# First block of a two-block model on one core: the gate and convolution projections computed by seven block products per pair of weight tiles, with gated sums kept in DRAM between phases

## The chip, the core and the metric

The kernel runs on one core of a Trainium2 chip. The metric is the device time of one execution in microseconds (us). The engines in the text: PE multiplies matrices (its weight loads are listed apart as PEld), DVE is the vector engine, ACT the scalar (activation) engine, POOL the GpSimd engine, SP the engine whose queue issues most loads. "hi" and "lo" are the two parts into which an fp32 operand is split, so that a product in reduced precision is made in three passes.

## The reference

Input x has 1024 tokens with 1024 features. The first block, cut to what the change touches:

```python
h = rmsnorm(x, norm_g)
q, k, v, z_att, gb, gc, u, z_conv, g_att, g_conv = split(h @ w_in)
att    = chunked_rel_attention(q, k, v, rel_bias)
y_att  = (att * silu(z_att)) @ w_att_out          # 512 -> 1024
vconv  = causal_depthwise_conv(gc * u)            # width 3
y_conv = (gb * vconv * silu(z_conv)) @ w_conv_out # 512 -> 1024
m = sigmoid(g_att) * y_att + sigmoid(g_conv) * y_conv
x = x + m @ w_out
```

rmsnorm(x, g) is x times a factor r per token (one over the root of the mean square) times the gain g. A final norm, a second block (a sparse-attention mixer, a cross attention and a gated feed-forward part, FFN, with 2816 hidden features) follow.

## The kernel before, in words

**Layout.** Activations lie transposed: 128 features on the partitions, 1024 tokens along the row, so 8 tiles make 1024 features. A weight tile is 128x1024 and holds eight 128x128 blocks, one for each tile of input features. `w` (line 173) loads one into the single buffer "wr"; ACT copies it to a hi tile ("wh"), DVE subtracts for the lo tile ("wl"). `dense_full` (line 202) makes 128 output features: 8 feature tiles (4 when the input has 512 features), two token halves and three passes (hi by hi, lo by hi, hi by lo: `mm3`, line 190), so 48 (or 24) matmuls of 128x512, into a PSUM tile "S".

**Buffers.** Named by tag, [128, 1024] fp32 each: U (32), P (6), PT (4), wr (1), wh and wl (2 each). PSUM: S (2 tiles, 1024 wide), T (2), A and D (1 each). A buffer is given out again in turn when its last reader is done. "spill" is a write to DRAM from POOL's queue (`dspill`, line 168), "reload" a read from there on SP's queue. A load may be tied to an earlier matmul (`ago`), so that it does not start too soon. Each engine takes its instructions in order; a scheduler sets that order from the program and its own estimates, except on PE inside `manual_schedule`, where the order of the program text holds.

**First block** (`block1`, line 675). The normed x (without the factor r: it is a row R over the tokens and is multiplied in afterwards, `times_R`) is held as 8 hi/lo pairs `hn` in 16 U buffers. Query, key, value and four pairs of heads are worked off; `z_gate` (line 578) makes for each pair the product att·silu(z) (`attg`) in hi/lo, which is spilled to DRAM and reloaded behind the last of them. Then:

- `rope_base` makes a sine and cosine table for the second block (into the tile "cs"), with 3 of ACT's changes of function table (sine, tanh) around it.
- `gates(28, "wao", attg, True)`: for each of 8 output tiles a gate product (w1[28+d], 48 matmuls), times R, tanh, and the y_att product (wao, 24 matmuls), combined to mt[d].
- a loop over 4 tiles with four products each (w1[16+d], [20+d], [12+d], [24+d]: gc, u, gb, z_conv), with the convolution and the gating between them, to `convg`.
- `gates(36, "wco", convg, False)`: the same for the convolution branch, added to mt[d].
- mt split to hi/lo (`ms`), and 8 products with wo1, to which x is added.

**The FFN of the second block** has another scheme, which the change takes over. Two weight tiles of 128 output features are done together. The 1024 input features are taken as two halves and the two output tiles as two, a 2x2 block product, and likewise the tokens in two halves of 512; sums of blocks are made first, so that seven products of 12 matmuls each (`product`, P1 to P7) take the place of eight: 84 matmuls instead of 96. `operands` (line 1473) makes the right-hand sums from the activations once (7 U tiles for each of 4 pairs of feature tiles), `left_x` and `left_y` (lines 1497, 1504) make the left-hand ones for every weight pair (on DVE and ACT, in wh, wl, PT and U buffers). `begin` runs P1 of a pair, `end` the others, with P1 of the next pair between P7 and P4; ACT or DVE takes partial results out of PSUM between them. In the FFN, R is multiplied in behind the products.

Of the kernel before, what the change touches and what calls it, by code (L numbers as in the profile page):

```python
# [98 lines left out]
class Kernel:  # L99
# [568 lines left out]
    def block1(self):  # L668
# [40 lines left out]
        self.rope_base()  # L709
        mt = [self.big("U" if d < 6 else "P") for d in range(8)]  # L710
        whole = slice(0, 1024)

        def gates(c0, wname, src, first):
            wy = None
            for d in range(8):
                g = self.dense_full(I["w1"][c0 + d], hn)
                th = self.times_R(g, whole, "P")
                self.act(th, th, AF.Tanh, scale=0.5)
                if d % 2 == 0:
                    wy = self.w(I[wname][d // 2])  # L720
                y = self.dense_full(None, src, w=wy, wo=(d % 2) * 512)
                if first:
                    self.stt(mt[d], th, 1.0, y, OP.add, OP.mult)
                else:
                    self.stt(th, th, 1.0, y, OP.add, OP.mult)
                    self.tt(mt[d], mt[d], th, OP.add)

        gates(28, "wao", attg, True)
        convg = []
        R2 = self.big("PT")  # L730
        self.act(R2, self.R, AF.Square)
        for d in range(4):
            gc = self.dense_full(I["w1"][16 + d], hn)
            u1 = self.big("PT")
            self.act(u1, gc)
            u = self.dense_full(I["w1"][20 + d], hn)
            self.tt(u1, u, u1, OP.mult)
            self.tt(u1, u1, R2, OP.mult)
            t0 = self.big("P")
            cw = lambda j: self.gvec[:, GV["cw1"] + 4 * j + d:GV["cw1"] + 4 * j + d + 1]  # L740
            self.act(t0, u1, AF.Identity, scale=cw(2), bias=self.gv("cb1", d))
            self.stt(t0[:, 1:], u1[:, :1023], cw(1), t0[:, 1:], OP.mult, OP.add)
            self.stt(t0[:, 2:], u1[:, :1022], cw(0), t0[:, 2:], OP.mult, OP.add)
            gb = self.dense_full(I["w1"][12 + d], hn)
            self.tt(t0, t0, gb, OP.mult)
            self.nc.gpsimd.tensor_tensor(t0, t0, self.R, op=OP.mult)
            z = self.times_R(self.dense_full(I["w1"][24 + d], hn), whole)
            th = self.big("P")
            self.act(th, z, AF.Tanh, scale=0.5)
            self.stt(th, th, 1.0, z, OP.add, OP.mult)  # L750
            self.tt(t0, t0, th, OP.mult)
            hi, lo = self.big("U", F32R), self.big("U", F32R)
            self.split(hi, lo, t0, scale=0.5)
            convg.append((hi, lo))
# [968 lines left out]
```

## Time and profile before

| | |
|---|---|
| median of 3 runs | 2506.16 us (2504.4 to 2506.25) |
| the profiled execution | 2509.58 us, of which 2507.8 us are the span of the trace; mean granted PE clock 0.976 of full speed |
| PE busy in the span | 2384.4 us, 95% |
| gates and convolution branch, before the wo1 products | 316.39 to 757.54 us of the span |
| wo1 products | 757.54 to 845.83 us |
| FFN, one weight pair (of 22) | 19.29 us |

A line of an engine's timeline reads: start in us, length in us, engine, line of the kernel, operation, output<-inputs by buffer name, shape, count, and in brackets the idle time before it and what ended it. A row of a window reads: the stretch, its length, then PE, PEld, DVE, ACT and POOL busy time with (xcount), the granted PE clock as a share of full speed, the busy share of the DMA engines and GB/s. A row of the chain of waits: start, length, what the program's end waited for. A group's row ends in "busy us, mean ns of one | idle before".

### The profile page before, as it was taken

To read this page: it belongs to the slowest core of one execution; us is meant where nothing else is said; L and a number is where in the kernel's file an instruction comes from. 1 tells how busy PE (TensorE), PEld (TensorE's weight loads), DVE (VectorE), ACT (ScalarE), POOL (GpSimd) and SP (SyncE) were. 2 spreads that over 40 slices of the span, in tenths; PEclk is the share of its full clock that TensorE was granted. 3 is DMA by queue.
4 is the path that set the end of the run, shared out by engine and by line. 5 is a ranking of instruction groups with operands and counts; after the bars stand their busy time and mean duration, and the time that the engine had idled before them with its cause. 6 is when DMAs were issued, how large, how long until landed. Compare 5 with 4: busy or idle time off the path is not lost.

```text
span 2507.8 us, 32225 instructions
## 1 busy us (share of the span) xinstructions
PE 2384.4 (95%) x12516; PEld 2024.4 (81%) x12516; DVE 1527.3 (61%) x2502; ACT 1157.8 (46%) x1949; POOL 200.8 (8%) x302
## 2 busy tenths in 40 slices
PE   8999999999999999967878999999999999999999
PEld 7887878888888889966777787887878888888887
DVE  5476732333434469778966886444578888875443
ACT  4455521121223247687766774344445544553231
POOL 0000000001000014321211111000000000000000
PEclk9999999999999999988989999999999999999999
DMA  4323321111113332225343324311422222225454
GB/s 138 99 66 112 104 92 51 50 43 51 42 59 118 108 101 66 70 81 164 114 142 107 94 67 164 114 59 51 151 84 76 85 89 80 76 85 184 168 185 143
DMA packets 82328, 246.52 MB, mean 98 GB/s; under 512 B 10368, under 2 KB 15872, under 8 KB 82176
## 3 DMA queue, kind: packets, MB, share of 16 engines
q1 hardware_dynamic: 68256, 195.48, 24.6%
q0 software_dynamic: 13488, 48.77, 5.3%
q8 instruction: 98, 1.61, 0.3%
q10 hardware_dynamic: 432, 0.23, 0.1%
q14 instruction: 54, 0.44, 0.1%
HBM read 171.03 MB, written 51.90 MB: 89 GB/s over the span
## 4 chain that ended last, share of the span: by engine, by line
PE 75%; DVE 9%; issue 6%; ACT 5%; DMA 3%; POOL 2%; SPq 0%; DVEq 0%; POOLq 0%; ACTq 0%
PE S L186 46%; PE D L186 9%; PE T L186 9%; PE A L186 7%; PE T L490 2%; ACT jka L130 2%; DVE U L133 2%; DMA U<-sp 1%; DVE P L133 1%; ACT P L130 1%; DVE P L483 1%; POOL st L218 1%; DVE jkd L1117 1%; ACT U L130 1%; DVE PT L133 1%
## 5 line engine op out<-in xcount | busy, mean ns | idle before, releaser
L186 PE MATMUL S<-U,wh 128*128 128x512 f32 x2624 | 831.7, 392 | 16.4 <-ACT U L130 8.4
L186 PEld LDWEIGHTS S<-U,wh 128*128 128x128 f32 x2624 | 495.2, 189 | 122.5 <-ACT U L130 8.4
L186 PE MATMUL S<-U,wl 128*128 128x512 f32 x1312 | 513.4, 391 | 2.8 <-DVE wl L133 2.8
L130 ACT ACTIVATE wh<-wr 128x1024 fp32r<-128x1024 f32 (+1 forms) x144 | 145.7, 1011 | 579.1 <-PE S L186 354.8
L186 PEld LDWEIGHTS S<-U,wl 128*128 128x128 f32 x1312 | 247.9, 189 | 56.9 <-DVE wl L133 4.7
L133 DVE TENSOR_TENSOR wl<-wr,wh 128x1024 fp32r<-128x1024 f32 (+1 forms) x144 | 167.5, 1163 | 193.1 <-ACT wh L130 192.9
L186 PE MATMUL D<-U,wh 128*128 128x512 f32 x752 | 261.8, 400 | 0.3 <-DVE U L133 0.2
L186 PE MATMUL S<-U,U 128*128 128x256 f32 (+6 forms) x1040 | 217.3, 336 | 14.5 <-DVE st L483 13.6
L186 PEld LDWEIGHTS S<-U,U 128*128 128x128 f32 x1040 | 161.0, 201 | 31.2 <-DVE st L483 14.3
L186 PEld LDWEIGHTS D<-U,wh 128*128 128x128 f32 x752 | 140.8, 189 | 27.4 <-DVE U L133 1.5
L186 PE MATMUL D<-U,wl 128*128 128x512 f32 x376 | 149.1, 396 | 0.4 <-DVE wl L133 0.4
L130 ACT ACTIVATE P<-P,st 128x640 f32<-128x640 f32 (+7 forms) x168 | 124.0, 739 | 40.4 <-DVE st L483 38.9
L186 PE MATMUL S<-wh,U 128*128 128x256 f32 x768 | 142.7, 288 | 0.0
L130 ACT ACTIVATE PT<-T 128x512 fp32r<-128x512 f32 (+4 forms) x208 | 110.3, 544 | 53.4 <-PE T L490 46.0
L186 PE MATMUL S<-U,PT 128*128 128x512 f32 x528 | 130.1, 395 | 0.0
L186 PEld LDWEIGHTS S<-wh,U 128*128 128x128 f32 x768 | 122.7, 196 | 0.0
L186 PE MATMUL T<-U,wh 128*128 128x512 f32 x352 | 119.0, 390 | 0.0
L186 PEld LDWEIGHTS S<-U,PT 128*128 128x128 f32 x528 | 99.1, 188 | 23.7 <-ACT jkd L130 0.2
L186 PE MATMUL A<-PT,U 128*128 128x256 f32 (+2 forms) x448 | 110.8, 340 | 5.2 <-ACT PT L130 1.9
L130 ACT ACTIVATE jka<-U,C 128x768 int8<-128x768 f32 (+2 forms) x96 | 99.7, 1039 | 34.1 <-DVE C L136 29.5
L133 DVE TENSOR_TENSOR PT<-T,PT 128x512 fp32r<-128x512 f32 (+1 forms) x160 | 101.6, 646 | 22.5 <-ACT PT L130 20.6
L133 DVE TENSOR_TENSOR P<-S,R 128x512 f32<-128x512 f32 (+1 forms) x46 | 39.8, 872 | 120.0 <-PE S L186 120.0
(296 smaller groups left out, 4144.2 us busy)
## 6 DMA issues: line engine op xcount, KB each, us to landing
U<-sp SPq DMA_DIRECT2D x65, 512.0 KB, 4.1
sp<-U POOLq DMA_DIRECT2D x53, 512.0 KB, 3.7
wr<-in_w SPq DMA_DIRECT2D x43, 512.0 KB, 3.3
U<-in_wf SPq DMA_DIRECT2D x43, 512.0 KB, 3.6
P<-sp SPq DMA_DIRECT2D x42, 512.0 KB, 4.4
sp<-P POOLq DMA_DIRECT2D x38, 512.0 KB, 2.9
U<-U SPq DMA_DIRECT2D x116, 128.0 KB, 2.3
wr<-in_wf SPq DMA_DIRECT2D x23, 512.0 KB, 3.6
```

The source lines that it names most:

```text
L130: return self.nc.scalar.activation(out, in_, f, **kw)
L133: return self.nc.vector.tensor_tensor(out, a, b, op=op)
L186: self.last = self.nc.tensor.matmul(out, l, r, start=start, stop=stop, skip_group_check=True)
L218: self.nc.gpsimd.tensor_tensor(y, v, self.mhalf[:, :n], op=OP.pow)
L483: self.nc.vector.tensor_tensor_reduce(pv, v, add.rearrange("p (n x) -> p n x", n=n), scale, BIG, OP.add, OP.min, nm)
L490: self.nc.tensor.transpose(T[:, j * 128:j * 128 + 128], b, self.ident)
L1117: self.nc.vector.tensor_scalar(self.junk["d"][:, :w], SD[i], C[:, j:j + 1].bitcast(F32), None, op0=OP.is_lt, op1=OP.add, accum_out=cnt[:, ...
```

## The change

The part of `block1` between z_gate and the wo1 products becomes a new method `gates(attg)`. It does these things:

- All 32 weight tiles of the gates and the convolution loop go through the seven-product scheme, as 16 pairs (28/29 to 34/35 for the attention gate; 16+d/20+d and 12+d/24+d for the convolution; 36/37 to 42/43 for its gate). Right-hand sums are made from x itself, loaded anew (8 tiles), times the gain and times R; for the first four feature tiles in one DVE instruction, for the others by an ACT scaling and a POOL multiply by R. `hn` is no longer needed there, and `times_R` goes.
- The y_att products (wao) stand first. While they run, the right-hand sums are made. Their results go out of PSUM by ACT, in halves through the tiles cs and jkd, and to DRAM (16 DMAs of 256 KB on SP's queue). For j=0 two S tiles are filled together, feature tile by feature tile.
- Gated sums (M, 8), convolution results (4) and six of the eight tanh tiles of the second gate are spilled and reloaded between the phases; the y_att results are reloaded (8).
- The y_conv products (wco) stand last, in the order j = 3, 2, 1, 0, and ms[d] is split as each is made. The wo1 products begin at feature tile 4 (`rot=4`).
- z_gate(3) keeps its hi/lo in SBUF; attg[1] is reloaded into P buffers, attg[2] into PT buffers.
- `rope_base` stands behind the pair loop. PE's order is that of the text for the whole part.

Rows in the program's order (neighbouring instructions that read alike share one): PE 11504 before and 11248 after, of which 64 new ones stand for two matmuls each, so that there are 192 matmuls fewer; DVE 2342 and 2504; ACT 1514 and 1635; POOL 267 and 283; SP 530 and 578. Everything up to the last z_gate, and everything behind the first wo1 product, stands in the same order as before on every engine. Lines of the kernel from 168 on move by three.

SP's queue at the start of the part, with the reloads of attg (names with numbers: sp291/292 are attg[0], sp447/448 attg[1], sp599/600 attg[2], sp681/682 attg[3]). Before:

```order
L158 DMA U683_3293<-sp291_1632 128x1024
L158 DMA U684_3294<-sp292_1634 128x1024
L158 DMA U685_3297<-sp447_2294 128x1024
L158 DMA U686_3298<-sp448_2296 128x1024
L158 DMA U687_3301<-sp599_2948 128x1024
L158 DMA U688_3302<-sp600_2950 128x1024
L158 DMA wr714_3437<-in_w1 128x1024
L158 DMA U689_3305<-sp681_3289 128x1024
L158 DMA U690_3306<-sp682_3291 128x1024
```

After:

```order
L158 DMA U681_3289<-sp291_1632 128x1024
L158 DMA U682_3290<-sp292_1634 128x1024
L158 DMA PT685_3297<-sp599_2948 128x1024
L158 DMA PT686_3298<-sp600_2950 128x1024
L158 DMA P683_3293<-sp447_2294 128x1024
L158 DMA P684_3294<-sp448_2296 128x1024
L158 DMA P687_3303<-in_xT 128x1024
L158 DMA P688_3305<-in_xT 128x1024
```

The reload of attg[3] is gone, attg[1] stands behind attg[2], and two tiles of x follow.

ACT at the same place (wh708 and wh711: the first wao tile; P679/P680 and U673: the tail of z_gate(3); S701: the first y_att result; U692, U695: right-hand sums). Before:

```order
L130 ACTIVATE wh711_3407<-wr710_3405 128x1024
L130 ACT_TABLE_LOAD
L130 ACTIVATE cs8_110<-PT694_3321 128x256
L130 ACT_TABLE_LOAD
L130 ACTIVATE P680_3283<-P679_3281 128x512
L130 ACT_TABLE_LOAD
L130 ACTIVATE cs8_110<-PT696_3331 128x256
L130 ACTIVATE PT765_4043<-R12_115 128x1024
L130 ACTIVATE U673_3221<-P680_3283 128x512
L130 ACTIVATE wh715_3439<-wr714_3437 128x1024
```

After:

```order
L130 ACTIVATE wh708_3403<-wr707_3401 128x1024
L130 ACTIVATE P680_3283<-P679_3281 128x512
L130 ACTIVATE U673_3221<-P680_3283 128x512
L130 ACTIVATE U692_3314<-P687_3303 128x512
L130 ACTIVATE P688_3305<-P688_3305,gvec1_63 128x1024
L130 ACTIVATE U695_3325<-P688_3305 128x1024
L130 ACTIVATE cs8_110<-S701_3337 128x512
L130 ACTIVATE jkd11_114<-S701_3337 128x512
```

The sine table is gone from here; the copies of S701 out of PSUM stand behind U695, which reads P688 after POOL has multiplied it by R.

DVE at the end of the part (before: P903, P912 the last gates, S913 the last y_conv result, P704 the last mt, wl936 the first wo1 tile; after: U1117 a reloaded tanh tile, S1130 the last y_conv result, U1116 the last gated sum, U1132 its lo part, wl1147 a wo1 tile). Before:

```order
L133 TENSOR_TENSOR P912_5679<-S911_5630,R12_115 128x1024
L133 TENSOR_TENSOR wl936_5750<-wr934_5747,wh935_5749 128x1024
L136 SCALAR_TENSOR_TENSOR P912_5679<-P912_5679,S913_5682 128x1024
L133 TENSOR_TENSOR P704_3346<-P704_3346,P912_5679 128x1024
L133 TENSOR_TENSOR wl944_5816<-wr942_5813,wh943_5815 128x1024
L136 SCALAR_TENSOR_TENSOR U929_5738<-P704_3346,U928_5737 128x1024
```

After:

```order
L136 SCALAR_TENSOR_TENSOR U1129_6071<-U1114_5967,U1128_6070 128x1024
L136 SCALAR_TENSOR_TENSOR U1117_5973<-U1117_5973,S1130_6074 128x1024
L133 TENSOR_TENSOR wl1147_6181<-wr1145_6178,wh1146_6180 128x1024
L133 TENSOR_TENSOR U1116_5971<-U1116_5971,U1117_5973 128x1024
L136 SCALAR_TENSOR_TENSOR U1132_6102<-U1116_5971,U1131_6101 128x1024
```

In both a wo1 tile's lo part stands in the chain from the last y_conv result to the last ms; the last one made is ms[7] before and ms[1] after.

The diff, without the removed loops of `block1` (they stand above) and without most of `left_y`, which gets the weight tile and the buffer tag as arguments and is now a generator in two steps:

```diff
+    def droom(self):
+        self.n += 1
+        return self.dr.tile([128, 1024], F32, name=f"sp{self.n}", tag=f"sp{self.n}", bufs=1)
...
-    def z_gate(self, p, hn, att, attg):
+    def z_gate(self, p, hn, att, attg, keep=False):
...
-        attg[p] = [self.dspill(x.bitcast(F32)) for x in (hi, lo)]
+        attg[p] = (hi, lo) if keep else [self.dspill(x.bitcast(F32)) for x in (hi, lo)]
...
-        drain(self.z_gate(3, hn, att, attg))
+        drain(self.z_gate(3, hn, att, attg, keep=True))
-        for p in range(4):
-            hl = [self.big("U", F32R) for _ in range(2)]
+        for p, tag in ((0, "U"), (1, "P"), (2, "PT")):
+            hl = [self.big(tag, F32R) for _ in range(2)]
...
+        with self.tc.manual_schedule(engines={mybir.EngineType.PE}):
+            ms = self.gates(attg)
...
-            ps = self.dense_full(I["wo1"][d], ms)
+            ps = self.dense_full(I["wo1"][d], ms, rot=4)
...
-    def left_y(self, f):
+    def left_y(self, f, ap, tag="U"):
...
+        add(s12, ("S1", "S2"), ("wh", "wl"))
+        yield
...
+    def gates(self, attg):
+        nc, I, R = self.nc, self.I, self.R
+        h = [slice(0, 512), slice(512, 1024)]
+        s2 = self.cs.rearrange("p s t d -> p (s t d)")
+        s3 = self.junk["d"].bitcast(F32)
+        w1, self.A, self.B = I["w1"], {}, [None] * 4
+        Y, M, TH, CV = {}, {}, {}, {}
+        def normed(x, k):
+            if k < 4:
+                self.stt(x, x, self.gv("norm", k), R, OP.mult, OP.mult)
+            else:
+                self.act(x, x, scale=self.gv("norm", k))
+                nc.gpsimd.tensor_tensor(x, x, R, op=OP.mult)
+            return x
+        for j in range(4):
+            x, y = [self.load(self.big("P"), I["xT"][j + 4 * z], self.ago(8000)) for z in range(2)]
+            w = self.w(I["wao"][j])
+            if j == 0:
+                self.B[j] = dict(self.operands(normed(x, j), lambda: normed(y, j + 4)))
+            if j == 0:
+                ps = [self.t("S", [128, 1024]) for _ in range(2)]
+                for k in range(4):
+                    for z in range(2):
+                        c = slice(z * 512 + k * 128, z * 512 + k * 128 + 128)
+                        for half in range(2):
+                            self.mm3(ps[z][:, h[half]], w[0][:, c], w[1][:, c], attg[k][0][:, h[half]],
+                                     attg[k][1][:, h[half]], k == 0, k == 3)
+            else:
+                ps = [self.dense_full(None, attg, w=w, wo=z * 512) for z in range(2)]
+            if j:
+                ops = self.operands(normed(x, j), lambda: normed(y, j + 4))
+                self.B[j] = dict(ops if j < 3 else [next(ops) for _ in range(3)])
+            for z in range(2):
+                d = Y[2 * j + z] = self.droom()
+                for half, y in enumerate((s2, s3)):
+                    self.act(y, ps[z][:, h[half]])
+                    nc.sync.dma_start(d[:, h[half]], y)
+        def sig_mid(n, g, a, c):
+            self.act(a[:, h[0]], c, AF.Tanh, scale=0.5)
+        def att_fin(n, g, a):
+            self.act(a[:, h[1]], a[:, h[1]], AF.Tanh, scale=0.5)
+            self.act(g, g, AF.Tanh, scale=0.5)
+            for d, x in ((2 * n + 1, a), (2 * n, g)):
+                y = self.load(self.big("P"), Y[d], self.ago(8000))
+                self.stt(y, x, 1.0, y, OP.add, OP.mult)
+                M[d] = self.dspill(y)
+        def u_mid(n, g, a, c):
+            self.tt(a[:, h[0]], c, g[:, h[0]], OP.mult)
+        def u_fin(n, g, a):
+            d = (n - 4) // 2
+            self.tt(a[:, h[1]], a[:, h[1]], g[:, h[1]], OP.mult)
+            t = CV[d] = self.big("P")
+            cw = lambda j: self.gvec[:, GV["cw1"] + 4 * j + d:GV["cw1"] + 4 * j + d + 1]
+            self.act(t, a, AF.Identity, scale=cw(2), bias=self.gv("cb1", d))
+            self.stt(t[:, 1:], a[:, :1023], cw(1), t[:, 1:], OP.mult, OP.add)
+            self.stt(t[:, 2:], a[:, :1022], cw(0), t[:, 2:], OP.mult, OP.add)
+        def z_mid(n, g, a, c):
+            t = CV["th"] = self.big("P")
+            self.act(t[:, h[0]], c, AF.Tanh, scale=0.5)
+            self.stt(t[:, h[0]], t[:, h[0]], 1.0, c, OP.add, OP.mult)
+        def z_fin(n, g, a):
+            d, t = (n - 5) // 2, CV["th"]
+            self.act(t[:, h[1]], a[:, h[1]], AF.Tanh, scale=0.5)
+            self.stt(t[:, h[1]], t[:, h[1]], 1.0, a[:, h[1]], OP.add, OP.mult)
+            self.tt(t, t, CV[d], OP.mult)
+            self.tt(t, t, g, OP.mult)
+            CV[d] = self.dspill(t)
+        def conv_fin(n, g, a):
+            self.act(a[:, h[1]], a[:, h[1]], AF.Tanh, scale=0.5)
+            self.act(g, g, AF.Tanh, scale=0.5)
+            for d, x in ((2 * (n - 12) + 1, a), (2 * (n - 12), g)):
+                TH[d] = x if d >= 6 else self.dspill(x)
+        todo = [(28 + 2 * j, 29 + 2 * j, sig_mid, att_fin) for j in range(4)]
+        for d in range(4):
+            todo += [(16 + d, 20 + d, u_mid, u_fin), (12 + d, 24 + d, z_mid, z_fin)]
+        todo += [(36 + 2 * j, 37 + 2 * j, sig_mid, conv_fin) for j in range(4)]
+        def begin(n):
+            c = self.t("S", [128, 512])
+            s1 = self.big("wr")[:, h[0]]
+            A = self.A[n][0]
+            self.product(c, A, "P1", True)
+            self.act(s1, c)
+            return n, A, c, s1
+        def end(n, A, c, s1):
+            mid, fin = todo[n][2:]
+            T = self.t("T", [128, 512])
+            g, a = self.big("P"), self.big("P")
+            o = self.t("DA"[n % 2], [128, 512])
+            self.product(o, A, "P2", True)
+            self.tt(g[:, h[0]], o, s1, OP.add)
+            self.product(c, A, "P6", False)
+            self.act(s2, c)
+            self.product(T, A, "P5", True)
+            self.product(c, A, "P7", False)
+            self.act(s3, c)
+            self.tt(a[:, h[1]], T, s3, OP.add)
+            nxt = begin(n + 1) if n < 15 else None
+            self.product(c, A, "P4", False)
+            mid(n, g, a, c)
+            self.product(T, A, "P3", False)
+            self.tt(g[:, h[1]], T, s2, OP.add)
+            fin(n, g, a)
+            return nxt
+        def conv_in(d):
+            t = self.load(self.big("P"), CV[d], self.ago(8000))
+            hi, lo = self.big("U", F32R), self.big("U", F32R)
+            self.split(hi, lo, t, scale=0.5)
+            return hi, lo
+        self.left_x(0, w1[28], "wr")
+        cur = begin(0)
+        left = self.left_y(0, w1[29], "P")
+        next(left)
+        self.B[3].update(ops)
+        drain(left)
+        for n in range(16):
+            if n < 15:
+                self.left_x(n + 1, w1[todo[n + 1][0]])
+                drain(self.left_y(n + 1, w1[todo[n + 1][1]]))
+            else:
+                convg = [conv_in(d) for d in range(4)]
+            cur = end(*cur)
+        self.rope_base()
+        ms = [None] * 8
+        if self.stop == "convg":
+            return convg
+        def ahead(j):
+            if j < 0:
+                return None
+            for d in (2 * j, 2 * j + 1):
+                M[d] = self.load(self.big("U"), M[d], self.ago(8000))
+                if d < 6:
+                    TH[d] = self.load(self.big("U"), TH[d], self.ago(8000))
+            return self.w(I["wco"][j])
+        w2 = [ahead(3), ahead(2)]
+        for j in (3, 2, 1, 0):
+            w = w2.pop(0)
+            for z in range(2):
+                d = 2 * j + z
+                y = self.dense_full(None, convg, w=w, wo=z * 512)
+                m, th = M[d], TH[d]
+                self.stt(th, th, 1.0, y, OP.add, OP.mult)
+                self.tt(m, m, th, OP.add)
+                tag = "PT" if j == 3 else "U"
+                hi, lo = self.big(tag, F32R), self.big(tag, F32R)
+                self.split(hi, lo, m, scale=0.5)
+                ms[d] = hi, lo
+            w2.append(ahead(j - 2))
+        return ms
```

More of the change, by code (lines that the diff above doesn't have):

```diff
@@ L166, in ago @@
         return self.hist[0][1]
+    def droom(self):
+        self.n += 1
+        return self.dr.tile([128, 1024], F32, name=f"sp{self.n}", tag=f"sp{self.n}", bufs=1)
     def dspill(self, src):
-        self.n += 1
-        dt = self.dr.tile([128, 1024], F32, name=f"sp{self.n}", tag=f"sp{self.n}", bufs=1)
+        dt = self.droom()
         self.nc.gpsimd.dma_start(dt, src)
@@ L708, in block1 @@
             return self.dump_hl(attg)
[L709 to L754, printed above, removed]
@@ L755, in block1 @@
-        if self.stop == "convg":
-            return self.dump_hl(convg)
-        gates(36, "wco", convg, False)
-        if self.stop == "m":
-            return self.dump(mt)
-        ms = []
-        for d in range(8):
-            tag = "PT" if d < 2 else "U"
-            hi, lo = self.big(tag, F32R), self.big(tag, F32R)
-            self.split(hi, lo, mt[d], scale=0.5)
-            ms.append((hi, lo))
+        with self.tc.manual_schedule(engines={mybir.EngineType.PE}):
+            ms = self.gates(attg)
@@ L1493, in operands, with left_x @@
                 yield n, (hi[:, c], lo[:, c])
-    def left_x(self, f, tag="U"):
-        x = self.load(self.big(tag), self.I["wf1"][22 + f])
+    def left_x(self, f, ap, tag="U"):
+        x = self.load(self.big(tag), ap)
         hi, lo = self.t("wh", [128, 1024], F32R), self.t("wl", [128, 1024], F32R)
@@ L1503, in left_x, with add @@
         self.A[f] = {n: (hi[:, c], lo[:, c]) for n, c in zip(("11", "12"), h)}, x
-    def left_y(self, f):
+    def left_y(self, f, ap, tag="U"):
         A, x = self.A[f]
         h = [slice(0, 512), slice(512, 1024)]
-        y = self.load(self.big("U"), self.I["wf1"][f])
-        s12, s4 = self.big("U"), self.big("U")
-        self.tt(s12[:, h[0]], y[:, h[0]], y[:, h[1]], OP.add)
-        self.tt(s12[:, h[1]], s12[:, h[0]], x[:, h[0]], OP.subtract)
-        self.tt(y[:, h[0]], x[:, h[0]], y[:, h[0]], OP.subtract)
-        self.tt(s4[:, h[0]], x[:, h[1]], s12[:, h[1]], OP.subtract)
-        for v, names, tags in ((s12, ("S1", "S2"), ("wh", "wl")), (y, ("S3", "22"), ("PT", "PT"))):
+        def add(v, names, tags):
             hi, lo = [self.t(n, [128, 1024], F32R) for n in tags]
@@ L1517, in left_y @@
             A.update((n, (hi[:, c], lo[:, c])) for n, c in zip(names, h))
+        y = self.load(self.big(tag), ap)
+        s12, s4 = self.big(tag), self.big(tag)
+        self.tt(s12[:, h[0]], y[:, h[0]], y[:, h[1]], OP.add)
+        self.tt(s12[:, h[1]], s12[:, h[0]], x[:, h[0]], OP.subtract)
+        add(s12, ("S1", "S2"), ("wh", "wl"))
+        yield
+        self.tt(y[:, h[0]], x[:, h[0]], y[:, h[0]], OP.subtract)
+        self.tt(s4[:, h[0]], x[:, h[1]], s12[:, h[1]], OP.subtract)
+        add(y, ("S3", "22"), ("PT", "PT"))
         u = self.big("PT", F32R)
```

9 lines of the change are left out of this document (5 added, 4 removed).

## The prediction

> **What bounds the kernel now.** I read the page first, then the chain of waits around the changed part, then windows.
>
> ```profile
> span 2507.8 us, 32225 instructions
> PE 2384.4 (95%) x12516; PEld 2024.4 (81%) x12516; DVE 1527.3 (61%) x2502; ACT 1157.8 (46%) x1949; POOL 200.8 (8%) x302
> PE 75%; DVE 9%; issue 6%; ACT 5%; DMA 3%; POOL 2%; SPq 0%; DVEq 0%; POOLq 0%; ACTq 0%
> ```
>
> PE is busy for 95% of the span and is 75% of the chain that ended last. The average alone says little, so here is the chain through the changed part, and the stage as windows:
>
> ```profile
> 329.19 5.21 DMA U<-sp
> 334.40 0.04 issue
> 334.44 511.39 PE S L186 x2243
> 845.86 1.23 DVE P L133
> ...
> 316.39:757.54 441.15, 437.38 (x1921) 361.34 (x1920) 150.88 (x134) 92.10 (x88) 14.11 (x6) 1.00 0.16 54
> ```
>
> From 334.4 to 845.8 us, 511 us without a break, the end waits for PE and nothing else; the only other piece is a reload of attg. In the changed part PE is busy 437.4 of 441.15 us, DVE 151, ACT 92: a matmul less is time less there, and the other engines have room. Now the rate of a matmul in this stage, and what was lost at its start:
>
> ```profile
> 341.16 0.62 PE L186 MATMUL S<-U,wh 128*128 128x512 f32 x2
> 343.88 0.62 PE L186 MATMUL S<-U,wh 128*128 128x512 f32 x2
> ...
> PE S L186 <- DMA U<-sp: 3.8, 2, 2.0
> ...
> 330.00:332.00 2.00, 0.80 (x4) 0.67 (x4) 0.00 (x0) 1.11 (x2) 0.00 (x0) 1.00 0.88 307
> 332.00:334.00 2.00, 0.39 (x2) 0.00 (x0) 0.00 (x0) 0.00 (x0) 0.00 (x0) 1.00 0.76 293
> 334.00:336.00 2.00, 1.56 (x5) 1.28 (x6) 0.00 (x0) 0.00 (x0) 0.00 (x0) 0.82 0.09 33
> 336.00:338.00 2.00, 2.00 (x6) 1.57 (x5) 0.00 (x0) 0.00 (x0) 0.00 (x0) 0.50 0.00 0
> 338.00:340.00 2.00, 2.00 (x8) 1.58 (x8) 0.62 (x1) 0.00 (x0) 0.00 (x0) 0.82 0.00 0
> ```
>
> The two timeline rows begin 2.72 us and twelve matmuls apart (four feature tiles, three passes): 2.72/12 = 0.2267 us each. 1920 of them would take 435.25 us; the stage took 441.15, so 5.9 us went at the start: PE waited 3.8 us for the reloads of attg, and the granted clock then fell to 0.82, 0.50 and 0.82. So a wait cost 5.9/3.8 = 1.55 times its own length.
>
> **The matmuls.** The program has 32 weight tiles by 48 = 1536 matmuls for gates and convolution; after it has 16 pairs by 84 = 1344. The 384 for wao and wco stay. Removed: 1536 x 0.2267 = 348.2 us. The price of a pair is in the FFN's chain, which runs the same scheme on the same buffers:
>
> ```profile
> 2080.83 8.32 PE S L186 x36
> 2089.15 2.80 PE T L186 x12
> 2091.95 2.72 PE A L186 x12
> 2094.67 2.72 PE S L186 x12
> 2097.39 2.73 PE T L186 x12
> 2100.12 8.32 PE S L186 x36
> ...
> 2080.83:2100.12 19.29, 19.29 (x85) 15.76 (x85) 15.63 (x19) 9.58 (x11) 0.53 (x1) 1.00 0.25 83
> ```
>
> Six pieces make 84 matmuls in 19.29 us, with no idle PE and DVE busy for 15.63. Added: 16 x 19.29 = 308.6 us; at 0.2267 each a pair would be 19.04, which I keep as the other bound (16 x 0.25 = 4.0 us less). Net: 308.6 - 348.2 = **-39.6 us**, all on PE, which sets the end.
>
> Can DVE and ACT follow? Prices:
>
> ```profile
> L133 DVE TENSOR_TENSOR wl<-wr,wh 128x1024 fp32r<-128x1024 f32 x46 | 56.2, 1223 | 28.4 <-ACT wh L130 28.3
> L133 DVE TENSOR_TENSOR P<-P,U 128x512 f32<-128x512 f32 x4 | 2.7, 686 | 0.0
> L130 ACT ACTIVATE wh<-wr 128x1024 fp32r<-128x1024 f32 x46 | 48.8, 1061 | 303.2 <-PE S L186 264.6 <-DMA wr<-in_wao 10.5 <-DMA wr<-in_wco 10.1
> L130 ACT ACTIVATE cs<-S 128x512 f32<-128x512 f32 x21 | 12.1, 576 | 0.0
> L746 POOL TENSOR_TENSOR P<-P,R 128x1024 f32<-128x1024 f32 x4 | 13.0, 3262 | 281.8 <-DVE P L133 281.8
> ```
>
> A new pair needs on DVE, for the left-hand sums, 4 x 0.69 + 3 x 1.22 + 0.69 = 7.1 us, for results 4 x 0.69 = 2.7, for the gating two to three full tiles, 2.4 to 3.7: 12.2 to 13.5 us, less than the FFN's 15.63 in the same period. ACT has some 8 us. So I cost these at nothing, hidden by PE's 19.3 us. The bound above is one half-width DVE instruction late in every pair, 16 x 0.69 = 11.0 us.
>
> Hidden by the same cover: POOL issues 16 more DMAs and SP 48, in a stage whose DMA share was 0.16. rope_base, moved behind the loop, lies under the wco products (192 x 0.2267 = 43.5 us), and its two or three table loads on ACT go from the critical start. Were that cover gone, each table load or full tile would cost about a full-width ACT instruction's 1.06 us.
>
> **The stall that goes.** attg[3] stays in SBUF, the others have their reloads issued earlier than the x tiles: **-5.9 us**, unless something is late in their place. Four things are.
>
> (a) The start. attg[1] stands behind attg[2] on SP's queue, and attg[2]'s PT buffer is free only after its last reader:
>
> ```profile
> 312.40 1.62 PE L186 MATMUL A<-PT,U 128*128 128x128 f32 x12 [0.58 <-DVE U L133]
> 306.39 2.73 SPq L158 DMA_DIRECT2D U<-sp  x6
> ```
>
> That reader is in the group starting at 312.40, about 313.2. SP issues one DMA per 2.73/6 = 0.45 us, so attg[1] goes out at about 313.8 and 314.2; at the burst rate of about 300 GB/s in the windows above, four transfers of 512 KB need 7 us from 313.2 at worst (320.2), and 5.21 us each as in the chain from 314.2 (319.4). PE needs them after 12 matmuls, 316.4 + 2.7 = 319.1. I take 0.5 us, between 0 and 3.
>
> (b) From wao j=0 to j=1. Both S tiles are full when 48 matmuls and (a) are done, 316.4 + 10.9 + 0.5 = 327.8. The order shows ACT's copies of S701 behind U695, and that behind POOL. From the last z_gate product at 316.4: its tail on DVE, four half-width (2.7) and one full (1.22) instruction, and two ACT halves (0.58 each), 321.5; then x by gain and R on DVE 1.22, U692 0.58, ACT's scaling 1.06, POOL 3.26, U695 1.06, two copies 1.15: 329.8 without hand-overs. PE waits about 2.2 us. With the clock's share as at the old stall, 1.55 x 2.2 = 3.4; I take **3.4**, between 0 and 5.
>
> On that share, the Trainium skill ("TensorE: Matmul & The Clock Gate", Part 1) puts the fall to half clock after an idle window of about 3.4 us. The trace disagrees: a window at 0.50 followed two waits that both were shorter. By the page (b) would be 2.2 and the sum 1.2 us lower.
>
> (c) From wao to the first pair: c's copy and the left-hand sums stand behind the last copies through cs and jkd. Two copies of 0.58 are about 1.2, I take **1.3**, between 0 and 3.
>
> (d) The start of wo1:
>
> ```profile
> 757.81 1.22 DVE L136 SCALAR_TENSOR_TENSOR P<-P,S 128x1024 f32<-128x1024 f32 x1 [3.14 <-PE S L186]
> 759.07 1.23 DVE L133 TENSOR_TENSOR P<-P,P 128x1024 f32<-128x1024 f32 x1
> 760.33 1.06 ACT L130 ACTIVATE U<-P 128x1024 fp32r<-128x1024 f32 x1 [1.21 <-DVE P L133]
> 761.42 1.23 DVE L136 SCALAR_TENSOR_TENSOR U<-P,U 128x1024 fp32r<-128x1024 f32 x1
> ```
>
> Before, this chain led to ms[7], read in the eighth place. After, it leads to ms[1], which with rot=4 is read in the sixth place, 15 x 0.2267 = 3.4 us after the last product. With wl1147 (1.22) in between, the chain has its hi part at 0.27 + 3 x 1.22 + 1.06 = 5.0 and its lo part at 6.2. PE waits 1.6 and, two matmuls later, 0.7: **2.3**, between 1 and 3.6 (with the clock's share).
>
> Sum of the four: 0.5 + 3.4 + 1.3 + 2.3 = 7.5. In all -39.6 - 5.9 + 7.5 = **-38.0 us**. The profiled execution took 2509.58 us, 1.8 beside its span, so 2471.6 in its terms; it is 3.4 above the median, which becomes 2506.2 - 38.0 = **2468**. wo1 from its second product on, and all behind it, is unchanged.
>
> **The rivals.**
>
> *A lock between DVE and POOL.* Rows from the mixer:
>
> ```profile
> 1253.12 2.88 POOL L1233 TENSOR_TENSOR U<-U,st 128x1024 f32<-128x1024 f32 x1
> 1254.24 1.78 DVE L133 TENSOR_TENSOR st<-C,st 128x1 int32<-128x1 int32 x1
> 1256.74 0.15 DVE L133 TENSOR_TENSOR st<-st 128x1 int32<-128x1 int32 x1
> ```
>
> A DVE instruction of one column took 1.78 us instead of 0.15 and ended when POOL's ended (1256.0). In the wao phase POOL multiplies four tiles by R at 3.26 us, and DVE has per j: 1.22 for x, 4 x 0.69, 0.69, three lo parts and wl at 1.22, 9.5 us of PE's 10.9. If DVE stands still for each multiply, j takes 12.8 us, 1.9 more, three times: +5.7, **2474**. Against it: the 3.26 us of these rows came when DVE was lightly used, and POOL can be the one that waits. The Trainium skill ("SBUF — State Buffer", Practical consequences) says that a DVE instruction with two SBUF inputs and a GpSimd instruction that reads SBUF exclude each other, the one that starts first holding it to its end. The trace agrees, 1.78 us against 0.15. Chance 0.14.
>
> *A late instruction in each pair.* The +11.0 above on the forecast: **2479**. For it: the fins come after P3, and the mids hold up the S tile. Against it: the FFN's period without idle PE. Chance 0.08.
>
> *Nothing late.* All four stalls hidden (-7.5), pairs at the plain rate (-4.0): **2457**; with stalls hidden alone 2461. Against it stands the order on ACT and DVE. Chance 0.11.
>
> *Slower.* The pair's P buffers. Every pair takes two or three of six, and they come free only when a spill from POOL's queue has landed, or a reload has been used. If g and a are had late, the first result cannot leave PSUM, and P2's successor waits, in each pair again. It decides from 38.0/16 = 2.4 us per pair; at 3 us it is +48, **2516**. For it:
>
> ```profile
> U<-sp SPq DMA_DIRECT2D x65, 512.0 KB, 4.1
> sp<-P POOLq DMA_DIRECT2D x38, 512.0 KB, 2.9
> ```
>
> a reload takes 4.1 us and a spill 2.9, and DVE waits in order behind the load, with the next pair's left-hand sums queued there. Against it: the FFN spills one P tile in every pair with the same buffers and loses nothing, and the reloads have 19 us. Chance 0.03.
>
> That the change does not do what it says cannot be: PE's order has the 192 matmuls fewer.
>
> **How the numbers follow.** The forecast with its stalls between their bounds (2463 to 2472) has 0.62; the rivals 0.14, 0.08, 0.11 and 0.03; 0.02 is left for cases between 2501 and 2511, within 0.2% of the median, which is about what a measurement of this kernel can tell from no change. The low end, 2457, is the case of nothing late. The high end adds to the forecast the clock's share on the other stalls (0.55 x 4.1 = 2.3), the lock (5.7) and the late instruction (11.0): 2487. Faster: 0.62 + 0.14 + 0.08 + 0.11 = 0.95; same 0.02; slower 0.03.
>
> **What would show it.** In the chain of the changed kernel, pairs between about 360 and 680 us with the period 19.29 and the pieces 8.32, 2.80 and 2.72; the stage from 316.4 to the first wo1 product some 403 us long in place of 441.15 (1728 matmuls). PE waits for ACT on S near 328, a dip of the clock behind it, and for ACT and DVE on U at the first wo1 product. DVE instructions of over 2 us beside POOL's multiplies would speak for the lock; waits of PE for DVE on T, A, D or S in every pair for the late instruction, and for P reloads or spills for the slower case. A period over 20 us, or a stall of over 4 us at any of the four places, would make the sum wrong.

## The result, and the profile after

The median of four runs is 2466.53 us (2465.67 to 2469.37) against 2505.28 us for the kernel before (2501.24 to 2506.25, four runs): 38.8 us less, ratio 0.985, 95% interval 0.9833 to 0.9867. Two more sets of runs (e3, whose edit left PE's order as it was, and e11, the changed kernel again), each beside runs of before on one chip, gave 0.9868 (0.9848 to 0.9887) and 0.9866 (0.9846 to 0.9887), so the gain is 31 to 39 us. The profiled execution took 2467.37 us. Its page:

```profile
span 2465.6 us, 32347 instructions
PE 2340.9 (95%) x12324; PEld 1982.7 (80%) x12324; DVE 1631.2 (66%) x2666; ACT 1231.2 (50%) x2070; POOL 211.1 (9%) x318
```

PE has 192 matmuls and 43.5 us of busy time less; DVE has 104 us more, and PE is 95% busy as before. The chain through one pair, with its window:

```profile
376.62 8.32 PE S L189 x36
384.95 2.80 PE T L189 x12
387.75 2.72 PE A L189 x12
390.47 2.72 PE S L189 x12
393.19 2.73 PE T L189 x12
...
376.62:395.92 19.30, 19.30 (x86) 15.78 (x85) 10.77 (x13) 7.68 (x10) 1.12 (x2) 1.00 0.46 171
```

These are the FFN's pieces to the hundredth, 19.30 us for 84 matmuls with no idle PE; DVE is busy for 10.77 of them (8.8 to 12.2 in the other pairs). So the pairs went as forecast. Where PE did wait in the part (its timeline, only the rows with a wait in brackets):

```profile
317.17 0.73 PE L189 MATMUL S<-P,wh 128*128 128x512 f32 x2 [0.44 <-DMA P<-sp]
...
326.78 0.50 PE L189 MATMUL S<-U,wh 128*128 128x512 f32 x1 [1.49 <-ACT jkd L130]
...
358.39 0.79 PE L189 MATMUL S<-U,wh 128*128 128x512 f32 x1 [3.64 <-ACT jkd L130]
...
669.57 3.06 PE L189 MATMUL S<-U,PT 128*128 128x512 f32 x12 [0.75 <-ACT jkd L130]
```

Four waits, 6.3 us. Two of the four that were forecast are there, (a) and (b); nothing waits at the first pair or at wo1; the longest, at 358.39, stands at a place that was not on the list: the last wao product (j=3, second tile), which needs the S tile that ACT has not yet emptied.

To compare runs without what varies in the rest of the program, I measure the part by itself, from the first matmul behind z_gate to the column sums behind wo1. Its ends in the kernel before and in the changed one, on PE's timeline:

```profile
316.39 0.39 PE L186 MATMUL S<-U,wh 128*128 128x512 f32 x1
...
850.77 3.57 PE L186 MATMUL A<-ones,P 128*128 128x1 f32 x16 [4.95 <-DVE P L133]
```

```profile
313.39 0.39 PE L189 MATMUL S<-U,wh 128*128 128x512 f32 x1
...
812.08 3.40 PE L189 MATMUL A<-ones,P 128*128 128x1 f32 x16 [4.95 <-DVE P L133]
```

534.38 us before and 498.69 after: 35.7 us less. The stage that the prediction put at some 403 us, up to the first wo1 product, took about 405 (313.39 to about 718.8). The span is 42.2 us shorter; the other 6.5 lie in code that the change does not touch (3.0 us ahead of the part, 3.5 behind), which is the size by which runs of one kernel differ.

### The profile page after: what moved, and what is told of

Same layout as the page of the kernel before. It is cut to its first block, busy times and chain, and to the rows that moved or that the text cites. A ratio compares the mean times of both kernels' runs of the same rounds, so it can differ in the third digit from the quotient of the medians.

```text
span 2465.6 us, 32347 instructions
## 1 busy us (share of the span) xinstructions
PE 2340.9 (95%) x12324; PEld 1982.7 (80%) x12324; DVE 1631.2 (66%) x2666; ACT 1231.2 (50%) x2070; POOL 211.1 (9%) x318
## 4 chain that ended last, share of the span: by engine, by line
PE 74%; DVE 11%; ACT 6%; issue 4%; DMA 2%; POOL 2%; SPq 0%; DVEq 0%; ACTq 0%; POOLq 0%
PE S L189 39%; PE T L189 12%; PE D L189 11%; PE A L189 9%; DVE U L133 2%; PE T L493 2%; ACT jka L130 2%; DVE P L133 1%; ACT P L130 1%; DMA U<-sp 1%; DVE PT L133 1%; DVE jkd L1067 1%; DVE P L486 1%; ACT U L130 1%; POOL st L221 1%
## 5 line engine op out<-in xcount | busy, mean ns | idle before, releaser
L189 PE MATMUL S<-U,wh 128*128 128x512 f32 x1792 | 582.7, 392 | 18.5 <-ACT U L130 8.4
L189 PEld LDWEIGHTS S<-U,wh 128*128 128x128 f32 x1792 | 338.5, 189 | 92.7 <-ACT U L130 8.4
L189 PE MATMUL S<-U,wl 128*128 128x512 f32 x896 | 351.3, 392 | 2.9 <-DVE wl L133 2.9
L189 PE MATMUL S<-U,U 128*128 128x256 f32 (+6 forms) x1040 | 216.0, 335 | 13.5 <-DVE st L486 12.7
L189 PE MATMUL S<-U,PT 128*128 128x512 f32 x912 | 224.8, 395 | 0.7 <-ACT jkd L130 0.7
L189 PEld LDWEIGHTS S<-U,PT 128*128 128x128 f32 x912 | 171.1, 188 | 41.9 <-ACT jkd L130 1.4
L189 PEld LDWEIGHTS S<-U,wl 128*128 128x128 f32 x896 | 169.4, 189 | 40.6 <-DVE wl L133 4.7
L130 ACT ACTIVATE wh<-U 128x1024 fp32r<-128x1024 f32 x73 | 77.4, 1060 | 114.1 <-PE T L189 51.9
L133 DVE TENSOR_TENSOR wl<-U,wh 128x1024 fp32r<-128x1024 f32 x73 | 89.2, 1222 | 65.4 <-ACT wh L130 65.4
L133 DVE TENSOR_TENSOR PT<-U,PT 128x1024 fp32r<-128x1024 f32 x74 | 67.7, 955 | 97.7 <-PE S L189 97.7
L189 PE MATMUL A<-U,wh 128*128 128x512 f32 x368 | 125.1, 390 | 0.0
```

The source lines that it names most:

```text
L130: return self.nc.scalar.activation(out, in_, f, **kw)
L133: return self.nc.vector.tensor_tensor(out, a, b, op=op)
L189: self.last = self.nc.tensor.matmul(out, l, r, start=start, stop=stop, skip_group_check=True)
```

## The experiments

My theory after this look: the gain is the matmuls and the old stall, as forecast; what it pays is mostly a lock between POOL and DVE that holds up ACT's queue. The rivals: DVE's own load makes the waits of the wao phase; part of the pairs' time is set by other engines; spills and reloads cost. The results, with the length of the part in the profiled execution:

| kernel | median us | ratio to before, 95% interval | part us |
|---|---|---|---|
| before | 2502 to 2505 | 1 | 534.38 |
| changed | 2466.53 | 0.985 (0.9833 to 0.9867) | 498.69 |
| e1 R on DVE | 2461.83 | 0.9831 (0.9814 to 0.9848) | 491.97 |
| e3 (order as changed) | 2471.19 | 0.9868 (0.9848 to 0.9887) | 500.22 |
| e4 before, attg[3] kept | 2496.40 | 0.9976 (0.9965 to 0.9987) | 528.41 |
| e5 eighth product | 2508.54 | 1.0026 (1.0016 to 1.0037) | 538.36 |
| e6 R all on POOL | 2473.53 | 0.9885 (0.9870 to 0.9899) | 502.21 |
| e7 wo1 in the text's order | 2473.19 | 0.9887 (0.9874 to 0.9900) | 502.69 |
| e8 spills and reloads twice | 2483.44 | 0.9926 (0.9915 to 0.9938) | 518.75 |
| e9 e1 and the last pair | 2465.62 | 0.9851 (0.9837 to 0.9866) | 492.07 |
| e10 e1 and attg's order | 2467.15 | 0.9860 (0.9844 to 0.9875) | 492.50 |
| e11 changed again | 2468.77 | 0.9866 (0.9846 to 0.9887) | 500.00 |
| e12 e1 again | 2464.49 | 0.9847 (0.9828 to 0.9867) | 492.00 |

**An eighth product in each pair.**

```diff
             self.product(o, A, "P2", True)
+            self.product(o, A, "P2", True)
```

> The changed kernel with one product of twelve matmuls (P2, written twice with the same result) more in each of the 16 pairs, so 96 matmuls per pair as in an eight-product scheme, and all else as changed. Theory 1 (the gain is the matmuls and nothing else in the pairs binds): 16 x 12 x 0.2267 = 43.5 us more than the changed kernel, about 2510, ratio to before 1.002, with a pair's period of 22.0 us. Theory 2 (DVE, ACT or reloads set part of the period, so more matmuls are partly free): less than 35 us more.

The part is 38.1 to 39.7 us longer than in the changed kernel, and the time is above that of the kernel before. The chain of a pair:

```profile
375.55 8.32 PE S L189 x36
383.87 2.80 PE T L189 x12
386.67 5.44 PE A L189 x24
392.12 2.72 PE S L189 x12
394.83 2.73 PE T L189 x12
397.56 2.56 PE S L189 x11
```

From 375.55 to 397.56 the period is 22.01, 2.71 more than 19.30, and 16 times that is 43.4, as theory 1 has it. Most of the rest of the difference is the wao phase: here PE waited 0.82 us before the last product instead of 3.64, with no slow clock behind. So in the pairs PE binds and nothing else does, and what they gain is the seven products in place of eight.

**The kernel before without the reload of attg[3].**

```diff
-        attg[p] = [self.dspill(x.bitcast(F32)) for x in (hi, lo)]
+        attg[p] = [hi, lo] if p == 3 else [self.dspill(x.bitcast(F32)) for x in (hi, lo)]
...
-        for p in range(4):
+        for p in range(3):
             hl = [self.big("U", F32R) for _ in range(2)]
```

> The kernel before with one part of the change alone: z_gate(3) keeps its hi and lo in SBUF, no spill and no reload of attg[3]. Theory 1 (the 5.9 us at the stage's start were the waits of 1.73 and 2.05 us for this reload and the slower clock behind them): 5 to 6 us less than before, ratio 0.9977. Theory 2 (the other reloads are as late, and PE waits for them instead): less than 2 us.

The median fell by 6.1 us, the part by 6.0, and windows that showed the dip are full:

```profile
334.00:336.00 2.00, 2.00 (x10) 1.65 (x10) 0.00 (x0) 0.00 (x0) 0.00 (x0) 1.00 0.00 0
336.00:338.00 2.00, 2.00 (x11) 1.65 (x10) 0.00 (x0) 0.00 (x0) 0.00 (x0) 1.00 0.00 0
```

PE is busy throughout at the full clock. The term of 5.9 us is shown, waits and clock together.

**The lock.** POOL's four multiplies by R in the changed kernel, and DVE's rows at those times:

```profile
321.67 3.00 POOL L1499 TENSOR_TENSOR P<-P,R 128x1024 f32<-128x1024 f32 x1 [36.42 <-ACT P L130]
327.84 2.41 POOL L1499 TENSOR_TENSOR P<-P,R 128x1024 f32<-128x1024 f32 x1 [3.18 <-ACT P L130]
337.32 2.83 POOL L1499 TENSOR_TENSOR P<-P,R 128x1024 f32<-128x1024 f32 x1 [7.07 <-issue]
349.92 6.36 POOL L1499 TENSOR_TENSOR P<-P,R 128x1024 f32<-128x1024 f32 x1 [9.77 <-ACT P L130]
```

```profile
328.75 2.59 DVE L133 TENSOR_TENSOR wl<-wr,wh 128x1024 fp32r<-128x1024 f32 x1 [1.01 <-ACT wh L130]
...
337.20 0.68 DVE L133 TENSOR_TENSOR PT<-P,PT 128x512 f32<-128x512 f32 x1
337.80 3.43 DVE L136 SCALAR_TENSOR_TENSOR P<-P,gvec,R 128x1024 f32<-128x1024 f32 x1
...
349.91 1.21 DVE L133 TENSOR_TENSOR U<-PT,U 128x1024 fp32r<-128x1024 f32 x1
...
353.38 0.68 DVE L133 TENSOR_TENSOR PT<-P 128x512 f32<-128x512 f32 x1
356.31 0.69 DVE L133 TENSOR_TENSOR PT<-P,P 128x512 f32<-128x512 f32 x1 [2.25 <-POOL P L1499]
```

At the second and third multiply POOL started ahead of these DVE instructions and DVE stood: 2.59 us for an instruction of 1.22, 3.43 for one of 1.28, each ending 1.1 us, about its own length, after POOL's. At the fourth a DVE instruction had started 0.01 us before POOL; DVE ran five back to back until 354.06, four of which started after POOL, and POOL ended 2.22 us after that, at 356.28: most of its 6.36 us is waiting. Then ACT, whose queue is in order:

```profile
356.31 1.06 ACT L130 ACTIVATE U<-P 128x1024 fp32r<-128x1024 f32 x1 [5.06 <-POOL P L1499]
...
357.75 0.59 ACT L130 ACTIVATE jkd<-S 128x512 f32<-128x512 f32 x1
```

ACT stood 5.06 us before the split of that tile, the two copies out of PSUM behind it ended at 358.34, and PE went on at 358.39. In e5 DVE had a gap of 0.12 us between two of these instructions (350.19 + 1.21 to 351.52), and POOL came in:

```profile
350.87 2.79 POOL L1499 TENSOR_TENSOR P<-P,R 128x1024 f32<-128x1024 f32 x1 [11.12 <-ACT P L130]
```

```profile
350.19 1.21 DVE L133 TENSOR_TENSOR U<-PT,U 128x1024 fp32r<-128x1024 f32 x1
351.52 2.69 DVE L133 TENSOR_TENSOR P<-P 128x512 f32<-128x512 f32 x1
```

There DVE stood (2.69 us for an instruction of 0.68) and PE lost 0.82 us. The instructions of this phase are the same in both kernels; what differs is which of the two stood, and how long POOL's multiply took. So the load of ACT and DVE alone does not make the 3.64 us. The Trainium skill ("SBUF — State Buffer", Practical consequences) says that a DVE instruction with two SBUF inputs and a GpSimd instruction that reads SBUF exclude each other, and that issue order decides who blocks. The traces agree on the first, in both directions. The order alone does not explain the fourth multiply, where four DVE instructions that started after POOL went ahead of it. Nor is the gap of 0.12 us the condition: at the third multiply POOL came while DVE was in the instruction from 337.20 to 337.88, the next was recorded from 337.80 on, and POOL still went first. Why POOL was passed over at the fourth stays open.

Two runs move the load to one side and to the other. R on DVE for all tiles:

```diff
-            if k < 4:
-                self.stt(x, x, self.gv("norm", k), R, OP.mult, OP.mult)
-            else:
-                self.act(x, x, scale=self.gv("norm", k))
-                nc.gpsimd.tensor_tensor(x, x, R, op=OP.mult)
+            self.stt(x, x, self.gv("norm", k), R, OP.mult, OP.mult)
```

> The changed kernel with the multiplication by R of the last four feature tiles in one DVE instruction, as for the first four: four ACT scalings and four POOL multiplies go, four DVE instructions of 1.27 us come. Theory 1 (POOL's multiplies and DVE's instructions shut each other out, and ACT's copies out of PSUM queue behind): PE's waits of 1.5 us near 325 and 3.6 us near 356 and the clock's dip behind the second go, 6 to 7 us less than the changed kernel, about 2460, ratio to before 0.982. Theory 2 (the phase is bound by DVE's own load, 9.5 us of 10.9 per j, and POOL relieves it): DVE rises to 10.8 of 10.9 us, the waits stay or grow, 2467 to 2475.

The waits for ACT in the wao phase are gone. What PE waits for on S in the part, and a window of the phase:

```profile
PE S L189 <- DMA P<-sp: 0.8, 1, 0.8
PE S L189 <- ACT jkd L130: 0.7, 1, 0.7
...
316.00:358.00 42.00, 41.15 (x179) 33.10 (x178) 39.11 (x46) 25.23 (x34) 0.00 (x0) 1.00 0.69 238
```

DVE is busy for 39.1 of 42 us there, and PE for 41.15 in place of 36.82. The part is 491.97 us, 6.7 less than the changed kernel and 8.2 less than its repetition e3 on the same chip. The edit also takes four scalings off ACT, so of the two waits that it removes only the longer one is tied to the lock, by e5; the 1.49 us came behind a multiply of 3.00 us, in a chain that the edit shortens. R on POOL for all tiles:

```diff
-            if k < 4:
+            if k < 0:
                 self.stt(x, x, self.gv("norm", k), R, OP.mult, OP.mult)
```

> The changed kernel with the multiplication by R on POOL for all eight feature tiles (and ACT's scaling for all): eight POOL multiplies in the wao phase in place of four, DVE has four instructions less. Theory 1 (POOL's multiplies and DVE's two-input instructions shut each other out, ACT's copies out of PSUM queue behind, and PE waits for these): more or longer waits of PE for ACT on S between 320 and 362 us than the 5.1 us of the changed kernel, 5 to 20 us more than the changed kernel, ratio to before 0.987 to 0.993. Theory 2 (DVE's load is what makes the waits): DVE has 1.2 us per j less, the waits fall, 2 to 5 us less than the changed kernel.

```profile
PE S L189 <- ACT jkd L130: 7.3, 4, 3.7
```

PE waits 7.3 us for ACT on S, 0.75 of it in the last pair and the rest, in three waits, in the wao phase; in the changed kernel it was 5.9 in all. The part is 502.2 us, 2 to 3.5 more than the changed kernel: theory 1's direction, though below its lower bound of 5. DVE had less to do and the waits grew, so DVE's load is not what makes them. In this run no multiply was passed over (none took more than 2.9 us); the longest wait, 3.71 us, came the other way round:

```profile
340.89 2.58 POOL L1499 TENSOR_TENSOR P<-P,R 128x1024 f32<-128x1024 f32 x1 [3.16 <-ACT P L130]
341.14 3.41 DVE L133 TENSOR_TENSOR U<-P,U 128x1024 fp32r<-128x1024 f32 x1
345.19 1.06 ACT L130 ACTIVATE U<-PT 128x1024 fp32r<-128x1024 f32 x1 [3.90 <-DVE PT L133]
346.78 0.79 PE L189 MATMUL S<-U,wh 128*128 128x512 f32 x1 [3.71 <-ACT jkd L130]
```

DVE stood for POOL (3.41 us for an instruction of 1.22), ACT stood for DVE's next result, and the copy out of PSUM was queued behind.

**Whether the gain of e1 is kept.** The changed kernel and e1 once more, without an edit, beside each other:

> The changed kernel once more, beside the next one on the same chip. Both theories: ratio to before between 0.984 and 0.987, the part 498 to 501 us long, POOL's fourth multiply either 6.4 us (then PE waits some 3.6 us) or 2.8 us (then about 0.8).

> The kernel of e1 once more, beside the changed kernel. Theory 1 (the part of 492 us in place of 499 is a gain of the whole): 5 to 7 us less than the changed kernel of the same call. Theory 2 (it is given back later): within 2 us of it.

In e11 POOL's fourth multiply took 6.36 us again and PE waited 3.62. Here e1 was 4.3 us below the changed kernel, a little under the 5 to 7 expected; beside e3, which is the changed kernel in other words (below), it was 9.4 below; the part was 492.0 against 500.0 us. The intervals of the times overlap here, so the size in the whole is 4 to 9 us and not better known. Its two medians are the lowest of the table, though by time alone they are not clear of e9 or of the changed kernel.

**wo1.** The first try put each wo1 product into a stretch of its own with PE in the text's order:

```diff
-            ps = self.dense_full(I["wo1"][d], ms, rot=4)
+            with self.tc.manual_schedule(engines={mybir.EngineType.PE}):
+                ps = self.dense_full(I["wo1"][d], ms, rot=4)
```

> The changed kernel with the wo1 products of the first block in the order of the text on PE, so that matmuls of the second wo1 product no longer stand among those of the first. Theory 1 (the wait at the last gated sum that the prediction priced at 2.3 us was filled by this interleaving): PE waits 1.6 and 0.7 us in the first wo1 product, 2 to 3.5 us more than the changed kernel with a dip of the clock. Theory 2 (the chain is shorter than I took it, so no wait was there to fill): 0, within 0.5 us of the changed kernel.

PE's order stayed what it was, the second product's matmuls among the first's, so this run says nothing on the question and serves as a repetition. The second put the whole loop into the stretch of `gates`:

```diff
         with self.tc.manual_schedule(engines={mybir.EngineType.PE}):
             ms = self.gates(attg)
...
-        for d in range(8):
+            for d in range(8):
```

> The changed kernel with the wo1 products inside the same stretch in which PE's order is that of the text; PE's first wo1 product then reads the last gated sum in the sixth place with nothing of the second product among it. Theory 1 (the wait that the prediction priced at 2.3 us was filled by matmuls of the second product): PE waits about 1.6 us for ACT and 0.7 us for DVE on U near 722 us; 2 to 3.5 us more, ratio 0.986. Theory 2 (no wait was there): no waits, ratio 0.985.

```profile
724.69 0.50 PE L189 MATMUL S<-U,wh 128*128 128x512 f32 x1 [1.23 <-ACT U L130]
725.95 1.22 PE L189 MATMUL S<-U,wh 128*128 128x512 f32 x2 [0.52 <-DVE U L136]
```

The two waits are there, at the places and for the engines that the prediction named for (d), 1.23 and 0.52 us where it said 1.6 and 0.7, and the part is 2.5 to 4.0 us longer. The windows around them:

```profile
722.00:724.00 2.00, 1.46 (x7) 0.85 (x5) 1.55 (x2) 0.42 (x1) 0.00 (x0) 1.00 0.29 76
724.00:726.00 2.00, 0.79 (x3) 0.35 (x3) 1.23 (x1) 0.64 (x1) 0.00 (x0) 0.96 0.47 186
726.00:728.00 2.00, 2.00 (x5) 1.61 (x6) 0.00 (x0) 0.00 (x0) 0.00 (x0) 0.50 0.00 0
728.00:730.00 2.00, 2.00 (x8) 1.58 (x7) 0.00 (x0) 0.00 (x0) 0.00 (x0) 0.68 0.00 0
```

After 1.75 us of idle time within 3 us the clock was 0.50, then 0.68: five matmuls in 2 us in place of ten.

**Spills and reloads twice.** Each new spill and reload (M, CV, TH, Y) goes through these:

```diff
+        def spill2(x):
+            self.dspill(x)
+            return self.dspill(x)
+        def load2(x, ap):
+            self.load(x, ap, self.ago(8000))
+            return self.load(x, ap)
```

> The changed kernel with each of its 18 new spills in the part (M, convolution results, tanh tiles) written twice, and each of the 26 reloads of these and of the y_att results read twice into the same buffer: 22 MB more. Theory 1 (spills and reloads are hidden by the 19.3 us of a pair's matmuls): within 3 us of the changed kernel, no wait of PE in the pairs. Theory 2 (they hold up the P buffers or DVE, as in the slower rival): PE waits in the four attention pairs and at the wco products, over 8 us more.

Theory 1 holds in the pairs up to the last: no waits there. From the last pair on it falls, at the wco products above all (PE's rows, then SP's queue):

```profile
672.62 3.07 PE L189 MATMUL S<-U,PT 128*128 128x512 f32 x12 [3.26 <-ACT jkd L130]
...
708.48 0.79 PE L189 MATMUL S<-U,wh 128*128 128x512 f32 x1 [8.20 <-ACT wh L130]
```

```profile
671.60 28.89 SPq L158 DMA_DIRECT2D U<-sp  x19
700.61 0.36 SPq L158 DMA_DIRECT2D wr<-in_wco  x1
```

The changed kernel has no wait at the wco products. Here the load of a wco weight left SP's queue only at 700.61, behind 19 reloads. The edit loads each tile twice into the same buffer, and between 640 and 730 us SP stood 32.3 us, in 14 waits, for such a reload to land before it could go on (none in the changed kernel); the DMA share (667 to 718 us) rose from 0.57 to 0.89. So the run does not tell too many bytes from a queue held up by the edit itself. The part grew by 18.5 to 20 us. The cover that the prediction named is real: in the pairs it held for twice the spills and reloads. How much there is at the end of the part stays open.

**Two small things on top of e1.** In the last pair P5 behind P7:

```diff
+            if n < 15:
+                self.product(T, A, "P5", True)
             self.product(c, A, "P7", False)
             self.act(s3, c)
+            if n == 15:
+                self.product(T, A, "P5", True)
```

> The changed kernel with the multiplication by R on DVE for all tiles, and in the last pair the product P5 behind P7, so that P4 does not wait for ACT's copy. Theory 1: PE's waits near 325 and 356 us and the one of 0.75 us near 669 go; 6 to 8 us less than the changed kernel, ratio to before 0.982. Theory 2 (the waits only move to later places): within 2 us of the changed kernel, ratio 0.985.

The part is 492.07 us, as in e1, so nothing is gained over it: the wait of 0.75 us is now at P7, for ACT's other copy, which P5 had covered. attg[1] ahead of attg[2]:

```diff
-        for p, tag in ((0, "U"), (1, "P"), (2, "PT")):
+        for p, tag in ((0, "U"), (1, "PT"), (2, "P")):
```

> R on DVE for all tiles as in e1, and attg[1] reloaded into PT buffers and ahead of attg[2], which goes to P. Theory 1 (the wait of 0.4 to 1.0 us at the start comes from the reload of attg[1] standing behind that of attg[2]): no wait of PE for DMA near 317 us, the part from the first wao product to the column sums behind wo1 about 491 us long (e1: 492.0, changed kernel 498.7); in the time within noise of e1. Theory 2 (the transfers themselves are late): attg[2] is late in its place, the wait stays.

The wait at the start is gone, but PE waits 1.21 us for DVE (a wl) at 351.89: DVE works there without a gap from 341.8 us on and reaches the wl only at 350.62. The part is 492.5 us.

## Why the prediction came right, step by step

- **The matmuls, -39.6.** Right: the pair's period and pieces are the FFN's, and e5 shows that the pairs are PE's. DVE's share of a pair was 8.8 to 12.2 us, at or below the low end of the 12.2 to 13.5 worked out. The rival of a late instruction in each pair, and the slower one on the P buffers, did not come: no pair but the last has a wait.
- **The old stall, -5.9.** Right, shown alone by e4.
- **(a), 0.5.** Right: 0.44, and 0.5 to 1.0 in the other runs; e10 shows that the place of attg[1]'s reload, with its buffer, is the cause.
- **(b), 3.4.** The mechanism was right, ACT's copies behind U695 behind POOL, but the size was off: 1.49 us. The step that failed is the clock's share: one wait of 1.5 us brought no dip, so nothing was to be added to the 2.2, which was itself 0.7 too long.
- **(c), 1.3.** Wrong in place and cause. Nothing waited at the first pair. What came was one product earlier: 3.64 us, and 36 matmuls at 10.06 us where 8.32 is usual elsewhere, 1.7 for the clock (0.58 and 0.57 in two windows; the row is of the chain):

```profile
358.39 10.06 PE S L189 x36
```

  The prediction had both halves, POOL's multiply in ACT's chain, costed for j=0 only, and the lock, as a rival in which DVE stands. The rival's sign came, two DVE instructions of 2.59 and 3.43 us beside POOL's multiplies, but PE lost nothing by these; it lost where POOL stood, since a PSUM tile waited for ACT behind POOL. e6 shows that DVE standing can cost as much. The rival's +5.7 is near the 5.3 that this cost (6.5 in e3 and e11), by another way.
- **(d), 2.3.** Not there. The chain was priced well, as e7 shows, but the wo1 products lie outside the stretch in which PE keeps the text's order, and the scheduler had put eight matmuls of the second product, and three more, into the gap.
- Not on the list: 0.75 us in the last pair, where no P1 of a next pair stands between P7 and P4.

Sum of the new waits: 0.44 + 1.49 + 3.64 + 1.7 + 0.75 = 8.0 us against 7.5 forecast. That the stalls' total came right is luck: (b) and (d) were too high by 1.9 and 2.3, (c) was too low by 4.0, and 0.75 was not on the list. The 45.5 us of matmuls and old stall, which make the forecast what it is, are not luck. -39.6 - 5.9 + 8.0 = -37.5 against -35.7 measured in the part. The other 1.8 us I cannot assign. The median moved by 38.8, but by 31.3 (e3) and 34.1 (e11) in the other two measurements, which fits the part's 34 to 36 us better.

## What to carry to other kernels

Where PE is busy without gaps, price a change by its matmuls, at the rate of the same scheme elsewhere in the same trace, and look for the losses at the seams between phases. An engine that multiplies for another can hold up a third, whichever of the two stands: follow each in-order queue to the PSUM tile that must be emptied behind it, for every round of a loop and not for the first alone. Before a wait is priced, look in the order for work that is placed into it.

## What the runs showed of the hardware

- A POOL multiply of 128x1024 took 2.41 us where it was first and 6.36 us when DVE ran five two-input instructions ahead of it. POOL got in at the end of the running DVE instruction when it had started 0.09 us (e3) to 0.78 us (e5) after that one, at the third multiply of these runs, and 0.68 us at the fourth of e5; it was passed over, at the fourth multiply of the changed kernel and of e3, e7, e8 and e11, when it had started 0.01 to 0.02 us after. No run shows why.
- The granted clock stayed full after single waits of 1.49 us (changed kernel) and of 1.39 and 1.43 us (e6). It fell to 0.50 after 1.23 and 0.52 us within 3 us (e7), and to 0.58 for some 4 us after 3.64 us:

```profile
358.00:360.00 2.00, 1.61 (x4) 1.32 (x5) 2.00 (x3) 1.91 (x3) 0.00 (x0) 0.58 0.67 249
360.00:362.00 2.00, 2.00 (x7) 1.57 (x6) 2.00 (x3) 2.00 (x4) 0.00 (x0) 0.57 0.14 53
```

How long a wait must be for a dip is not settled by these rows, nor is its length: behind nearly the same wait (3.62 to 3.67 us) the 36 matmuls took 10.12 us in e7 and 11.14, 11.19 and 11.34 in e3, e11 and e8. That is most of the 1.3 to 1.5 us by which the part is longer in e3 and e11 than in the changed kernel.
